# Second gate of the linear attention as a third seven-product block product, with adding DMAs for the weight sums

## The chip, the cores and the metric

The kernel runs on one NeuronCore of a Trainium2 chip. The metric is the device time of one execution in microseconds (us). TensorE (PE) multiplies matrices into PSUM; VectorE (DVE) and ScalarE (ACT) work elementwise on SBUF and PSUM; GpSimd (POOL) works on SBUF and issues DMAs; SyncE (SP) only issues DMAs. PEld is TensorE's loading of weights. All engines run their own instruction streams in order and wait for each other through semaphores.

## The reference, cut to what matters

One transformer block in float32 on 512 tokens of width 1024. One large projection gives all inputs; the change concerns the gate `z_ma`, which scales the output of the gated linear attention.

```python
n = rmsnorm(h, g_mix[l])
proj = n @ w_in[l]
(gq, gk, gv, gr, z_gf, z_gb, cq, ckv, kr, z_ma, z_mb) = jnp.split(proj, SPLIT_IDX, axis=-1)
y_gla = gla_branch(gq, gk, gv, gr, z_gf, z_gb, ...)     # ends with: rmsnorm(o, g_gla) * silu(gr)
y_mla = mla_branch(cq, ckv, kr, positions, ...)
merged = jax.nn.sigmoid(z_ma) * y_gla + jax.nn.sigmoid(z_mb) * y_mla
h = h + merged @ w_out[l]
m = rmsnorm(h, g_mlp[l])
h = h + jnp.square(jax.nn.relu(m @ w_ff1[l])) @ w_ff2[l]
```

`gr`, `gv` and `z_ma` are each 512 x 1024 (x 1024 inner). `gq` and `gk` are 512 wide (four heads of 128), `z_mb` is 1024 wide.

## The kernel before

**Precision.** Every float32 operand is split into a high part in the type fp32r (ACT, a copy) and a low part (DVE, source minus high part). A product of two operands is then three matmuls (`mm3`, line 430: high-high, high-low, low-high). `split` (435) is the pair of operations; `halves` (558) gives the two tiles for a weight block, of which there are four pairs (128 x 1024 each).

**Two ways to project.** A plain projection (`proj_begin`, `proj_run`) takes 128 columns of `w_in`: eight inner blocks of `mm3` over 512 tokens, 24 matmuls; its result stands with features on the partitions and tokens along the row. `gr` and `gv` instead go through `Seven` (1028): the 512 x 1024 times 1024 x 1024 product is cut in 2 x 2 blocks and computed with seven block products in place of eight (the Strassen-Winograd scheme). A block product is a 256 x 512 by 512 x 512 product, again 24 matmuls (four inner blocks, two token blocks, three terms), and its result has tokens on the partitions. The left sums (of the tokens' activations) are made once (`x_sums`, 998, on POOL; `split_sums`) and shared. The right sums (of weight blocks) are made by DVE in `less` (1043), subtracting one 128 x 1024 tile from another, two tiles per sum, four sums per block product. Before that, `load` (1033) brings all four weight blocks, two tiles of 512 KB each, over SP's queue. `right_split` splits a sum into halves. `multiply` (1076) runs the products and evacuates them: products 1, 5 and 6 are copied from PSUM by ACT into the rows c11, c22 and c12, products 2, 3 and 7 are added onto them by DVE. `sinks` (1102) hands finished rows on: `gr_rows` makes silu(gr) into `g1`, `gv_rows` makes the split values `v`.

**The gate before.** `z_ma` is computed by eight plain projections (`begin_za`, 1486). `za_gate` (1125) multiplies the result by the token rows' norm `R` (DVE), takes tanh (ACT) and scales and shifts by the gain `gla_gain` (ACT, bias and scale), since sigmoid(x) = (1 + tanh(x/2))/2. The linear attention's output of a head, gated by `g1` in `gla_gated`, is transposed in `gla_turn` (1151) and there multiplied by that gate (DVE).

**The order of the work.** From `nc.keep()` (1478) to `nc.flush` (2441) nothing is emitted at once: all operations are recorded, and `Due.order` (295) lays them out. It gives each operation a cost (`Work.cost`, 158) and a landing delay, works out a latest time for each from the order of the matmuls in the program, and then picks for each engine the ready operation that is due first. TensorE may take a matmul out of its order if that is due less than 6 us after the first one outstanding. Tiles of tags `u2` (24 buffers), `u4` (30), `wh`/`wl` (4) and the PSUM tags `mm` and `at` (4 banks each) put further limits on the order, since a new tile waits for the last use of an old one.

**Around the change.** The recorded part begins with the two sevens (gr, then gv). `prepare` for a product stands two steps ahead of it in the program. Filling projections (zb4, the gate and rotary-key projection zk, gq1, gk1, zb5) stand between products. Then come the heads h = 0, 1, 2 of the linear attention in a loop (1575): transposes of the keys (`turned`), `queries`, `scores`, one za projection, `values` (kv), `states` (a chain over four blocks of tokens, on ACT and DVE), another za projection, the output product `out`, squares and gating, the next head's q and k projections, and `gla_turn`. The gates' logarithms, scans and exponentials for the next head run meanwhile. The last head (1617) is mixed with the latent projections ckv and cq and the rotary parts, and with za6 and za7. Attention, the output product and the feed-forward part follow; these already form their weight sums with DMAs that add onto a tile (`nc.gpsimd.dma_start(..., accum_op=ALU.add)`), which POOL issues.

The steps of the sevens, before:

```python
SEVEN = (1, 2, 5, 6, 3, 7, 4)
steps = [(a, m) for a in range(2) for m in SEVEN]
```

Of the kernel before, what the change touches and what calls it, by code (L numbers as in the profile page):

```python
# [141 lines left out]
class Work:  # L142
    def __init__(self, engine, name, args, named):
# [8 lines left out]
        self.big = [n for x, n in zip(views, sizes) if not any(x is o for o in outs) and n > 4]  # L152
# [5 lines left out]
    def cost(self):  # L158
# [8 lines left out]
        if self.engine == "scalar":  # L167
            table = self.func not in (None, AF.Copy, AF.Identity, AF.Square)
            return 0.085 + 0.00086 * n + (0.02 if table else 0) + (0.11 if "accum_out" in self.named else 0)
        if self.engine == "vector":  # L170
            if self.name == "tensor_scan" or "scan" in self.name:
# [21 lines left out]
class Script:  # L193
# [4 lines left out]
    def __init__(self, nc, after):  # L198
        self.nc, self.after = nc, after
        self.kept, self.slots, self.last, self.used, self.count = None, {}, {}, {}, 0  # L200
        for e in self.ENGINES:
            setattr(self, e, Queue(self, e))
# [5 lines left out]
    def takes(self, held):  # L208
        held.real()
        if held.bufs is not None:  # L210
            here = self.slots.setdefault(held.kind, [])
            if len(here) == held.bufs:
                here.remove(min(here, key=lambda h: self.used.get(h, -1)))
            here.append(held)

    def told(self, work):
        self.count += 1
        for s in work.outs + work.ins:
            self.used[s[0]] = self.count
# [27 lines left out]
class Due:  # L247


    def __init__(self, todo, slots, head=0.0, tables=None):  # L250
# [4 lines left out]
        for i, w in enumerate(todo):  # L255
            for s in w.outs + w.ins:
                users.setdefault(s[0], []).append(i)
        wrote, read, seen, past = {}, {}, set(), {}
# [36 lines left out]
    def order(self):  # L295
# [4 lines left out]
            (9.4 if w.engine == "gpsimd" and w.bytes > 4e5 else 2.2) if w.is_dma else 0.13 for w in todo  # L300
# [30 lines left out]
        table = None  # L331
        self.idle = 0.0
        for _ in range(n):
            best = None
            for e in Script.ENGINES:
                among = open_[e]
                if e == "tensor" and among:
                    among = [i for i in among if late[i] < late[pe[-1]] + 6.0]
# [3 lines left out]
                i = min((i for i in among if ready[i] <= t + 0.1), key=lambda i: (late[i], i))  # L342
# [41 lines left out]
def tile_block(ctx: ExitStack, tc: tile.TileContext, t, out: bass.AP):  # L384
# [607 lines left out]
    SEVEN = (1, 2, 5, 6, 3, 7, 4)  # L992
# [5 lines left out]
    def x_sums():  # L998
        add = nc.gpsimd.tensor_tensor
        half = KD // 2  # L1000
        for p in range(half):
            a, b = xraw[p], xraw[p + half]
            y = u2(f"xy{p}")
            add(y[:, LO], a[:, HI], b[:, HI], op=ALU.add)
# [6 lines left out]
        for p in range(half):  # L1011
# [3 lines left out]
            add(z[:, HI], b[:, LO], x_y[p][:, HI], op=ALU.subtract)  # L1015
# [12 lines left out]
    class Seven:  # L1028
        def __init__(self, col, name, sink):
            self.col, self.name, self.sink = col, name, sink  # L1030
            self.blocks, self.right = [None] * 4, {}

        def load(self, x):

            self.blocks[x] = [u4(f"{self.name}w{x}{g}", F32, (P, 2, S)) for g in range(2)]
            for g in range(2):
                r = ((x // 2) * 4 + 2 * g) * P
                c = self.col + (x % 2) * S
                nc.sync.dma_start(
                    self.blocks[x][g], w_in[r : r + 2 * P, c : c + S].rearrange("(k p) w -> p k w", p=P)  # L1040
                )

        def less(self, dst, x, y):
            for g in range(2):
                nc.vector.tensor_tensor(
                    self.blocks[dst][g], self.blocks[x][g], self.blocks[y][g], op=ALU.subtract
                )
# [12 lines left out]
        def right_split(self, m, g):  # L1060
            x = {1: 0, 2: 2, 5: 0, 6: 0, 3: 3, 7: 1, 4: 2}[m]
# [14 lines left out]
        def multiply(self, m):  # L1076
# [5 lines left out]
            elif m == 5:  # L1082
                self.zs = [ps("at", f"{self.name}z{rb}") for rb in range(2)]
# [11 lines left out]
            if m in (1, 5, 6):  # L1095
                for acc, c in zip(accs, {1: self.c11, 5: self.c22, 6: self.c12}[m]):
                    nc.scalar.activation(c, acc, AF.Copy)
            elif m in (2, 3, 7):
                for acc, c in zip(accs, {2: self.c11, 3: self.c12, 7: self.c22}[m]):
                    nc.vector.tensor_tensor(c, acc, c, op=ALU.add)  # L1100

        def sinks(self, m):
# [3 lines left out]
            elif m in (2, 3, 7):  # L1106
                for rb, c in enumerate({2: self.c11, 3: self.c12, 7: self.c22}[m]):
# [15 lines left out]
    za_gates, held = {}, {}  # L1123
# [27 lines left out]
    def gla_turn(h):  # L1151

        half, at = h // 2, (h % 2) * GDV
        for dv in range(2):
# [6 lines left out]
            y = za_gates.pop(f)  # L1161
            nc.vector.tensor_tensor(y, tp, y, op=ALU.mult)
# [323 lines left out]
    def begin_za(f):  # L1486
        return begin(C_ZA + f * P, f"za{f}")
# [8 lines left out]
    def finish_zb(f, begun):  # L1496
        gated(proj_run(begun, xT), f"b{f}")


# [3 lines left out]
        (1, 2): (lambda: begin_qk(1, 0), lambda w: finish_qk(1, 0, w)),  # L1503
    }
    steps = [(a, m) for a in range(2) for m in SEVEN]
# [5 lines left out]
    for n, (a, m) in enumerate(steps[:-4]):  # L1511
        ahead = steps[n + 2]
        if a == 0:
# [956 lines left out]
```

## Time and profile before

| | us |
|---|---|
| median of 3 runs | 751.42 (750.8 to 752.75) |
| the profiled execution's own time | 752.12 |
| its span | 750.4 |
| TensorE's mean granted clock in it | 0.995 of full speed |

All instructions go through one helper line (L230), so groups are told apart by the names of the tiles. A group's row shows: engine, operation, out<-in, partitions x elements and type, count, busy time and mean duration in ns of one, then the engine's idle time just ahead and what ended it. Names: gr, gv, za, zb, gq, gk, ckv, cq with an h or l at the end are weight halves; grw, gvw the weight blocks; grx, grz, gvx, gvz accumulators of the sevens; kv the state products, st the states, glaNo the output product of head N, tr the tanh for silu. In the sections on the chain a piece is its start, its length and the engine.

### The profile page before, as it was taken

The numbers are of one execution on the slowest core, as the hardware profiler recorded it, in microseconds if no ns is written. First come the engines' busy times: TensorE is split into PE (matmuls) and PEld (weight loads), VectorE is DVE, ScalarE is ACT, GpSimd is POOL, SyncE is SP. The second block draws the span as 40 slices with busy tenths as digits, with TensorE's granted clock in tenths as the row PEclk, the third lists the DMA queues.
The fourth block names the chain that finished last, engine by engine and source line by source line (L and its number), as shares of the span: only waits on it lengthen the run. The fifth ranks groups of instructions, "written<-read, shape, count | busy, mean of one in ns | idle before, by whom it ended". The sixth has DMA issues, their size and how long they took to land.

```text
span 750.4 us, 11537 instructions
## 1 busy us (share of the span) xinstructions
PE 737.1 (98%) x4256; PEld 648.3 (86%) x4256; DVE 618.0 (82%) x920; ACT 503.7 (67%) x831; POOL 198.0 (26%) x243
## 2 busy tenths in 40 slices
PE   8999999999999999999999999999999999999996
PEld 6888788888888888899888899889988998889985
DVE  6699997887788486999997899857986798778885
ACT  7466649597776366988965768645873597458754
POOL 1540002113212104137743202322122211312433
PEclk9999999999999999999999999999999999999998
DMA  9931211413332316129975549998989897988992
GB/s 311 344 110 49 77 29 28 113 36 81 82 85 57 50 43 165 39 81 237 236 219 85 140 113 216 217 214 205 211 177 217 203 206 179 212 219 195 198 167 112
DMA packets 105176, 111.79 MB, mean 149 GB/s; under 512 B 15792, under 2 KB 75200, under 8 KB 105120
## 3 DMA queue, kind: packets, MB, share of 16 engines
q1 hardware_dynamic: 80976, 74.59, 32.9%
q0 software_dynamic: 23856, 35.94, 29.0%
q8 instruction: 33, 0.54, 0.3%
q10 hardware_dynamic: 288, 0.52, 0.2%
q14 instruction: 23, 0.19, 0.1%
HBM read 107.37 MB, written 2.10 MB: 146 GB/s over the span
## 4 chain that ended last, share of the span: by engine, by line
PE 85%; DVE 7%; ACT 3%; POOL 2%; issue 1%; DMA 1%; SPq 0%; POOLq 0%; DVEq 0%; ACTq 0%
PE mb L230 22%; PE ab L230 16%; PE za L230 6%; PE zb L230 4%; PE wox L230 3%; PE f L230 3%; PE gvx L230 3%; PE first L230 2%; PE grx L230 2%; PE cq L230 2%; PE gq L230 2%; PE gk L230 2%; PE ckv L230 1%; PE gvz L230 1%; PE woz L230 1%
## 5 line engine op out<-in xcount | busy, mean ns | idle before, releaser
L230 POOL DMA_DIRECT2D ms<-in_w_ff x37 | 47.3, 1372 | 115.5 <-DVE hl3l L230 37.5
L230 POOL DMA_DIRECT2D w1s<-in_w_ff x18 | 22.7, 1264 | 94.0 <-DVE hl0l L230 38.9
L230 DVE TENSOR_TENSOR h<-h,ab 128x512 f32<-128x512 f32 x48 | 31.7, 682 | 5.5 <-PE ab L230 5.5
L230 ACT ACTIVATE row<-row 128x512 f32<-128x512 f32 x49 | 30.7, 626 | 1.9 <-DVE row L230 1.0
L230 PE MATMUL av<-pT,v 128*128 128x256 f32 x192 | 28.2, 290 | 0.6 <-DVE pT L230 0.6
L230 PE MATMUL s<-kbuf,q 96*128 96x512 f32 x96 | 28.6, 409 | 0.0
L230 PEld LDWEIGHTS av<-pT,v 128*128 128x128 f32 x192 | 24.7, 191 | 1.2 <-DVE pT L230 0.8
L230 ACT ACTIVATE e<-s,top 128x512 f32<-128x512 f32 x32 | 21.9, 686 | 5.5 <-DVE top L230 5.2
L230 PE MATMUL mb<-four,hl0h 128*128 128x256 f32 x128 | 23.4, 284 | 0.1
L230 DVE TENSOR_REDUCE top<-s 128x1 f32<-128x512 f32 x32 | 21.5, 682 | 1.0 <-PE s L230 0.8
L230 DVE TENSOR_TENSOR pT<-tp,pT 128x512 fp32r<-128x512 f32 x32 | 21.5, 681 | 0.7 <-ACT pT L230 0.7
L230 DVE TENSOR_TENSOR hl3l<-ms,hl3h 128x1024 fp32r<-128x1024 f32 x13 | 15.9, 1224 | 7.0 <-ACT hl3h L230 6.8
L230 ACT ACTIVATE row<-mb 128x512 f32<-128x512 f32 x28 | 16.3, 582 | 7.3 <-PE mb L230 7.3
L230 PE MATMUL mb<-four,hl3h 128*128 128x256 f32 x112 | 20.5, 284 | 0.4 <-ACT row L230 0.4
L230 PEld LDWEIGHTS mb<-four,hl0h 128*128 128x128 f32 x128 | 20.1, 192 | 0.8 <-ACT hl2h L230 0.5
L230 PE MATMUL tp<-ident,e 128*128 128x128 f32 x128 | 19.5, 275 | 1.3 <-DVE pT L230 1.2
L230 ACT ACTIVATE hl3h<-ms 128x1024 fp32r<-128x1024 f32 x13 | 13.7, 1056 | 10.2 <-PE ab L230 4.6
L230 DVE TENSOR_TENSOR hl1l<-ms,hl1h 128x1024 fp32r<-128x1024 f32 x12 | 14.7, 1224 | 7.0 <-ACT hl1h L230 6.8
L230 PE MATMUL mb<-m,hl2h 128*128 128x256 f32 x112 | 20.4, 283 | 0.0
L230 PE MATMUL mb<-four,hl2h 128*128 128x256 f32 x112 | 20.4, 283 | 0.0
L230 PEld LDWEIGHTS tp<-ident,e 128*128 128x128 f32 x128 | 14.9, 140 | 5.5 <-PE s L230 1.5
L230 ACT ACTIVATE pT<-tp 128x512 fp32r<-128x512 f32 x32 | 19.0, 594 | 0.9 <-PE tp L230 0.8
(1097 smaller groups left out, 2815.4 us busy)
## 6 DMA issues: line engine op xcount, KB each, us to landing
ms<-in_w_ff POOLq DMA_DIRECT2D x37, 512.0 KB, 6.9
w1s<-in_w_ff POOLq DMA_DIRECT2D x18, 512.0 KB, 6.6
ms<-in_w_ff SPq DMA_DIRECT2D x16, 512.0 KB, 4.9
w1s<-in_w_ff SPq DMA_DIRECT2D x15, 512.0 KB, 4.7
w<-in_w_out POOLq DMA_DIRECT2D x10, 512.0 KB, 7.7
wf0f<-in_w_ff SPq DMA_DIRECT2D x10, 512.0 KB, 5.8
wf1f<-in_w_ff SPq DMA_DIRECT2D x10, 512.0 KB, 5.9
wf2f<-in_w_ff SPq DMA_DIRECT2D x10, 512.0 KB, 5.3
```

What stands on the lines that cost most here:

```text
L230: return call(*map(real, work.args), **{k: real(v) for k, v in work.named.items()})
```

## The change

- A third `Seven` for `z_ma` (named za) stands between gr and gv; its sink `za_rows` takes tanh by token rows, with the norm as ACT's scale, and multiplies 1 + tanh into `g1` (DVE). The eight plain za projections and `za_gate` go. `gla_turn` now only scales by the gain: ACT for one of a head's two parts, DVE for the other.
- The weight sums of all three sevens are formed by adding DMAs on POOL's queue (`by = "dma"`), onto B11 (three sums) and B22 (one). Block B12 has no tile of its own any more. The signs of the left sums and of the evacuations follow: product 3 is now copied into c12 and product 6 subtracted from it.
- The seven's inner order is now 1, 2, 5, 3, 6, 7, 4, and the list of steps interleaves the last products of a block with the first of the next. The accumulators of products 5 and 3 take banks of the tag `mm` instead of `at`.
- The fillers gq1 and gk1 stand in the last seven. zb5 moves into the first head; the second za projection's place in a head is taken by the next q projection; the first za place stays empty in heads 1 and 2. The first head's gate work stands in the last two steps of gv.
- The planner: new cost formulas, ACT's landing delay 0.145, TensorE may reach 20 us ahead instead of 6, ties within 0.05 us instead of 0.1, the activation table is known from the start, and tile slots are followed only for tiles with recorded uses.

```diff
 class Work:
+        sources = [*args[1:], *(x for k, x in named.items() if k != "accum_out")]
+        self.big = [x for x in sources if isinstance(x, View) and x.cells.size > 4]
+        self.from_psum = any(x.held.tag in ("mm", "at") for x in self.big)
...
         if self.engine == "scalar":
-            return 0.085 + 0.00086 * n + (0.02 if table else 0) + (0.11 if "accum_out" in self.named else 0)
+            more = (0.03 if table else 0) + (0.1 if "accum_out" in self.named and n > 256 else 0)
+            return more + (0.217 + 0.000543 * n if self.from_psum else 0.09 + 0.000857 * n)
...
-            extra = 0.055 if self.name == "scalar_tensor_tensor" and not self.psum else 0
-            return 0.07 + extra + (0.00105 if two or self.psum or self.name == "tensor_reduce" else 0.00066) * n
+            if self.name == "scalar_tensor_tensor":
+                return 0.125 + 0.00105 * n if not self.psum else 0.17 + 0.00085 * n
+            return 0.065 + (0.00105 if two or self.psum or self.name == "tensor_reduce" else 0.00066) * n
...
-                    among = [i for i in among if late[i] < late[pe[-1]] + 6.0]
+                    among = [i for i in among if late[i] < late[pe[-1]] + 20.0]
...
-                i = min((i for i in among if ready[i] <= t + 0.1), key=lambda i: (late[i], i))
+                i = min((i for i in among if ready[i] <= t + 0.05), key=lambda i: (late[i], i))
...
     class Seven:
-        def less(self, dst, x, y):
-            for g in range(2):
-                nc.vector.tensor_tensor(
-                    self.blocks[dst][g], self.blocks[x][g], self.blocks[y][g], op=ALU.subtract
-                )
+        def more(self, dst, x):
+            for g in range(2):
+                to = self.blocks[dst][g]
+                if self.by == "dma":
+                    nc.gpsimd.dma_start(to, self.rows(x, g), accum_op=ALU.add)
+                else:
+                    nc.vector.tensor_tensor(to, to, self.blocks[x][g], op=ALU.add)
 
         def right_sums(self, m):
             if m == 5:
-                self.less(0, 1, 0)
+                self.more(B11, B12)
             elif m == 6:
-                self.less(0, 3, 0)
-            elif m == 3:
-                self.less(2, 2, 0)
+                self.more(B11, B22)
             elif m == 7:
-                self.less(1, 3, 1)
+                if self.by == "dma":
+                    self.more(B22, B12)
+                else:
+                    self.more(B12, B22)
+            elif m == 4:
+                self.more(B11, B21)
...
             elif m == 5:
-                self.zs = [ps("at", f"{self.name}z{rb}") for rb in range(2)]
+                self.zs = [ps("mm", f"{self.name}z{rb}") for rb in range(2)]
...
-            if m in (1, 5, 6):
+            if m in (1, 5, 3):
...
-            elif m in (2, 3, 7):
+            elif m in (2, 6, 7):
...
-    def za_gate(f, acc):
-
-        z = u2(f"za{f}")
-        nc.vector.tensor_tensor(z, acc, R, op=ALU.mult)
-        nc.scalar.activation(z, z, AF.Tanh, scale=0.5)
-        gain = gla_gain[:, f : f + 1]
-        nc.scalar.activation(z, z, AF.Identity, bias=gain, scale=gain)
-        za_gates[f] = z
+    def za_rows(i, half, src, dst):
+        nc.scalar.activation(dst, src, AF.Tanh, scale=r_half[:, i : i + 1])
+        g = g1[i, half]
+        nc.vector.scalar_tensor_tensor(g, dst, 1.0, g, op0=ALU.add, op1=ALU.mult)
...
-            y = za_gates.pop(f)
-            nc.vector.tensor_tensor(y, tp, y, op=ALU.mult)
+            y = u2(f"y1{f}")
+            gain = gla_gain[:, f : f + 1]
+            if dv:
+                nc.vector.tensor_scalar(y, tp, gain, None, op0=ALU.mult)
+            else:
+                nc.scalar.activation(y, tp, AF.Copy, scale=gain)
...
-    sevens = [Seven(C_GR, "gr", gr_rows), Seven(C_GV, "gv", gv_rows)]
-    for x in (0, 2, 1, 3):
+    sevens = [Seven(C_GR, "gr", gr_rows, "dma"), Seven(C_ZA, "za", za_rows, "dma"), Seven(C_GV, "gv", gv_rows, "dma")]
+    for x in (B11, B21, B22):
         sevens[0].load(x)
...
-    steps = [(a, m) for a in range(2) for m in SEVEN]
+    steps = [(0, 1), (0, 2), (0, 5), (0, 3), (0, 6), (1, 1), (0, 7), (1, 2), (0, 4), (1, 5), (1, 3), (1, 6),
+             (2, 1), (1, 7), (2, 2), (1, 4), (2, 5), (2, 3), (2, 6), (2, 7), (2, 4)]
...
+        if a < 2:
+            for x in {2: (B11,), 5: (B21,), 6: (B22,)}.get(m, ()):
+                sevens[a + 1].load(x)
...
     for h in range(GH - 1):
         lin.turned()
         lin.queries()
         lin.scores()
-        if h:
-            w_b = begin_za(2 * h + 1)
-        acc = proj_run(w_a, xT)
+        if h == 0:
+            finish_zb(5, w_a)
...
         lin.states(coefs)
         gate.sums("f")
         if h < 2:
+            finish_qk(h + 2, 0, w_a)
             w_k, lows = begin_late(C_GK + (h + 2) * P, f"gk{h + 2}")
         else:
+            ckv_.run(0)
             ckv_.begun[1], lows = begin_late(C_CKV + P, "ckv1")
         gate.sums("b")
-        past, acc = acc, proj_run(w_b, xT)
         os = lin.out()
...
-    za_gate(6, proj_T(C_ZA + 6 * P, "za6"))
     lin.values()
     lin.states(coefs)
     cq = cq_.normed()
-    za_gate(7, proj_T(C_ZA + 7 * P, "za7"))
```

More of the change, by code (lines that the diff above doesn't have):

```diff
@@ L199, in __init__ @@
         self.nc, self.after = nc, after
-        self.kept, self.slots, self.last, self.used, self.count = None, {}, {}, {}, 0
+        self.kept, self.slots, self.last = None, {}, {}
         for e in self.ENGINES:
@@ L210, in takes @@
         if held.bufs is not None:
[L211 to L214, printed above, removed]
+            self.slots.setdefault(held.kind, []).append(held)
     def told(self, work):
-        self.count += 1
-        for s in work.outs + work.ins:
-            self.used[s[0]] = self.count
         if self.kept is not None:
@@ L330, in order @@
         shares = [w.shares() for w in todo]
-        table = None
+        table = 1
         self.idle = 0.0
@@ L1510, in tile_block, with prepare @@
     begun = {}
-    for n, (a, m) in enumerate(steps[:-4]):
-        ahead = steps[n + 2]
-        if a == 0:
-            for x in {3: (0,), 7: (2, 1), 4: (3,)}.get(m, ()):
-                sevens[1].load(x)
-        if steps[n + 1] in fillers:
+    for n, (a, m) in enumerate(steps):
+        ahead = steps[n + 2] if n + 2 < len(steps) else None
+        def prepare():
+            if ahead:
+                sevens[ahead[0]].prepare(ahead[1])
+        if a < 2:
+            for x in {2: (B11,), 5: (B21,), 6: (B22,)}.get(m, ()):
+                sevens[a + 1].load(x)
+        if n + 1 < len(steps) and steps[n + 1] in fillers:
             begun[steps[n + 1]] = fillers[steps[n + 1]][0]()
@@ L1525, in tile_block @@
             nc.gpsimd.dma_start(pos_i, t["positions"][0].partition_broadcast(P))
-        if (a, m) == (0, 4):
+        if (a, m) == (0, 7):
             z_chunk_finish(z_acc)
             split_gates()
+        if (a, m) == (2, 7):
+            gate = Gates(0)
+            gate.logs()
+        if (a, m) == (2, 4):
+            gate.sums("f")
+            gate.exps("f")
+            gate.sums("b")
+            gate.exps("b")
         if (a, m) in fillers:
             sevens[a].product(m)
-            sevens[ahead[0]].prepare(ahead[1])
+            prepare()
             rest = fillers[a, m][1](begun.pop((a, m)))
@@ L1600, in tile_block @@
         gate.exps("b")
-        za_gate(2 * h + 1, acc)
         gla_gated(h, os, rs)
```

83 lines of the change are left out of this document (27 added, 56 removed).

## The prediction

> **What bounds the kernel now.** I read the busy table first, then the chain of waits, then busy time by stage, then the groups and pieces that the change touches.
>
> ```profile
> span 750.4 us, 11537 instructions
> PE 737.1 (98%) x4256; PEld 648.3 (86%) x4256; DVE 618.0 (82%) x920; ACT 503.7 (67%) x831; POOL 198.0 (26%) x243
> PE 85%; DVE 7%; ACT 3%; POOL 2%; issue 1%; DMA 1%; SPq 0%; POOLq 0%; DVEq 0%; ACTq 0%
> ```
>
> TensorE is busy for 737.1 of 750.4 us and holds 85% of the chain. So only two things can move the time: the number of matrix products, and what opens or closes a gap between them. The stages say where gaps could open (columns: stretch, its length, then busy time and count of PE, weight loads, DVE, ACT, POOL, then clock, DMA share, GB/s).
>
> ```profile
> 43.40:146.00 102.60, 102.39 (x451) 84.29 (x450) 94.40 (x111) 65.33 (x86) 11.16 (x20) 1.00 0.22 59
> 146.00:297.20 151.20, 151.20 (x824) 131.11 (x823) 114.87 (x220) 106.21 (x200) 32.79 (x62) 1.00 0.29 73
> 297.20:381.00 83.80, 81.86 (x554) 73.07 (x553) 77.56 (x134) 72.48 (x160) 43.12 (x50) 1.00 0.65 164
> 360.00:381.00 21.00, 19.67 (x140) 17.25 (x140) 20.13 (x37) 18.97 (x43) 16.97 (x19) 1.00 0.98 255
> 480.00:730.00 250.00, 250.00 (x1576) 227.03 (x1575) 200.41 (x264) 155.78 (x208) 60.54 (x51) 1.00 0.94 201
> 730.00:750.40 20.40, 13.65 (x72) 11.62 (x70) 11.49 (x19) 8.99 (x20) 8.09 (x12) 0.89 0.28 103
> 297.20:750.40 453.20, 443.50 (x2818) 400.15 (x2816) 378.35 (x545) 304.63 (x501) 135.25 (x134) 0.99 0.79 180
> ```
>
> From 43.4 to 146 run the two seven-product blocks (gr and gv); from 146 to 297.2 the four heads of the linear attention with the eight za projections as filling; then attention. In the linear stage TensorE has no gap at all, with DVE at 114.87/151.20 = 76% and ACT at 70%. Attention, with DVE at 92.5% and ACT at 86.5%, leaves TensorE idle for 1.94 us of 83.8 (2.3%); its last quarter, DVE at 95.9%, for 1.33 of 21 (6.3%). The granted clock is 1.00 in all stages that the change touches, so no term below is a clock.
>
> **The change, part by part.**
>
> *Matrix products.* The chain shows one projection or one of the seven products as 24 matmuls:
>
> ```profile
> 43.75 5.44 PE grx L230 x24
> ...
> 149.43 5.47 PE za L230 x24
> 154.90 2.15 PE kv L230 x18
> 157.05 5.47 PE za L230 x24
> 162.52 3.59 PE gla0o L230 x30
> 166.11 5.47 PE gq L230 x24
> ```
>
> Eight za projections of 24 matmuls go, seven products of 24 come. One unit is 5.44 us, so TensorE loses 8 - 7 = 1 unit: **-5.44 us**. This is on the path, since TensorE is. No other matmul or transpose is added.
>
> *Work of DVE and ACT.* Rows (out<-in, shapes, count, busy us, mean ns, idle before):
>
> ```profile
> L230 DVE TENSOR_TENSOR gvw<-gvw,gvw 128x1024 f32<-128x1024 f32 x8 | 9.8, 1220 | 0.1
> L230 DVE TENSOR_TENSOR grw<-grw,grw 128x1024 f32<-128x1024 f32 x8 | 9.4, 1219 | 0.0
> L230 DVE TENSOR_TENSOR za<-za,R 128x512 f32<-128x512 f32 x8 | 5.5, 686 | 1.0 <-PE za L230 1.0
> L230 DVE TENSOR_TENSOR za<-y,za 128x512 f32<-128x512 f32 x8 | 5.3, 685 | 0.2
> L230 DVE TENSOR_TENSOR gv20l<-gvw,gv20h 128x1024 fp32r<-128x1024 f32 x1 | 1.2, 1218 | 0.0
> L230 DVE SCALAR_TENSOR_TENSOR grb<-tr,grb 128x512 f32<-128x512 f32 x2 | 1.3, 689 | 0.0
> L230 DVE TENSOR_SCALAR mf<-gatef,gvec 128x512 f32<-128x512 f32 x4 | 3.0, 748 | 0.6 <-PE gatef L230 0.6
> L230 ACT ACTIVATE za<-za,gla_gain 128x512 f32<-128x512 f32 x8 | 6.5, 813 | 0.2
> L230 ACT ACTIVATE za<-za 128x512 f32<-128x512 f32 x8 | 5.0, 626 | 0.6 <-DVE za L230 0.5
> L230 ACT ACTIVATE tr<-grb,r_half 128x512 f32<-128x512 f32 x2 | 1.3, 708 | 0.0
> L230 ACT ACTIVATE za2h<-za2f 128x1024 fp32r<-128x1024 f32 x1 | 1.1, 1062 | 0.1
> ```
>
> In the seven-product stage DVE loses the 16 differences of weights (9.8 + 9.4 = 19.2 us), the lows of za0, za1 (they lie before 146, about 2 x 1.2) and of zb5 (1.2), and gains 14 lows of the za block at 1.22 (17.1), 6 additions and 8 gate products at 0.69 (9.6): 94.4 - 22.8 + 26.7 = 98 us. TensorE there has 102.4 + 7 x 5.44 - 5.44 (zb5 moves on to the first head) = 135 us. DVE falls from 92% to 73%. ACT gains 14 highs at 1.06, 6 copies of accumulators (bounded by 0.6 to 0.8, the two rows za<-za and za<-za,gla_gain) and 8 tanh at 0.71 and loses 3 highs: 65 + 15 + 4 + 6 - 3 = 87 of 135 us. Neither bounds; all of it lies beside the products.
>
> In the linear stage the filling goes: TensorE 151.2 - 8 x 5.46 + 5.44 = 113 us. DVE loses six lows (7.3), eight scalings (5.5), six turned products (4.1; the last head's two lie in attention), and gains zb5's low (1.2) and three scalings out of PSUM at 0.75 (2.2; the other half goes to ACT): 114.9 - 16.9 + 3.4 = 101.4 us, **90% of TensorE's time instead of 76%**. ACT: 106.2 - 6.5 - 5.0 - 6.3 + 1.1 + 2 = 91.5, 81%. This is where a gap must be expected. Between the two rows for density (76%: no gap; attention's 92.5%: 2.3% of gap) 89.8% reads as 1.9% of 113 us: **+2.2 us**. Bounds: 0 (the row of before; no gain is possible in a stage without a gap) and 6.3%, the densest quarter of attention, 7.1 us. I take 2.2 because attention, with its chains of transpose, split and evacuation, is the row most like it.
>
> *The adding DMAs.* 24 transfers of 512 KB through POOL (four sums of two halves, three blocks) come; of the plain loads 18 stay for the blocks against 16 and eight for za.
>
> ```profile
> ms<-in_w_ff POOLq DMA_DIRECT2D x37, 512.0 KB, 6.9
> w1s<-in_w_ff POOLq DMA_DIRECT2D x18, 512.0 KB, 6.6
> gvw<-in_w_in SPq DMA_DIRECT2D x8, 512.0 KB, 6.1
> L230 POOL DMA_DIRECT2D ms<-in_w_ff x37 | 47.3, 1372 | 115.5 <-DVE hl3l L230 37.5 <-DVE hl0l L230 34.2 <-DVE hl1l L230 17.0
> DMA to landing us min/median/max: 3.7/6.6/15.4
> ```
>
> An issue costs POOL 1.37 us, 33 us in all, beside only 11 us of other POOL work in that stage. A sum then takes 1.4 + 6.9 us where DVE took 1.22, and it has to wait until the split before it has read the block. Is it in time? There are four pairs of halves and a product uses two, so the split for a product starts when the product two places ahead frees its half. For the tightest pair, product 5 and then 6 with one between: if 5 starts at t, its second half is split by t - 5.4 + 1.06 + 1.22 = t - 3.2, the first by t - 5.9. Product 6 starts at t + 10.9 and needs its first half split (2.3 us) by then, so the sum may take until t + 8.6: 14.5 us from the issue, against 6.9. **Cost 0.** The cover is the two products between; if it were gone, each microsecond beyond 14.5 would cost one, three times. The feed-forward stage supports the value: 250 us at 201 GB/s and 60 us of POOL, most of it such transfers, without a gap on TensorE, while the new stage would move some 41 x 0.52 MB in 135 us, 160 GB/s. Behind a waiting add on POOL stand the next add, the clearing of the scan rows and the small gate copies; the next add is the only urgent one, and one product of delay (5.4) still leaves 12.3 under 14.5. On SP's queue the loads of the next block wait for free tiles ahead of zb and gq weights; there were 16 + 8 such loads before and 18 now, so I cost it at 0 too.
>
> *The order elsewhere.* The new cost formulas, the window of 20 us for TensorE and the new tie limit lay every stage after the marker anew. From 297.2 to 730 TensorE idles 9.7 - 6.75 = 2.95 us; a new order could win or lose about half of it: -1.5 to +1.5, taken as 0. Swapping products 6 and 3, the changed signs and the bank for product 5 change no count.
>
> **Sum.** The profiled execution took 752.12 us, 0.70 above the median of the runs shown (751.42). 752.12 - 5.44 + 2.2 = 748.9; less 0.70: **748.2 us**. Its own range, with the order elsewhere, is 746.5 to 750.
>
> **The rivals.**
>
> *Everything stays covered.* No gap opens in the linear stage: 752.12 - 5.44 - 0.70 = 746.0. For it: the planner may now reach 20 us ahead for a ready matmul, and the next stage (zb6, cq) has DVE to spare. Against: 90% is close to attention's density. Chance 0.22.
>
> *The linear stage gets as tight as the end of attention.* Gap 7.1 us, 746.0 + 7.1 = 753.1. For it: per head the products shrink by about 10.9 us but the chain of scans, exponentials and states doesn't. Against: DVE has slack before (73%) and after. Chance 0.18. The Trainium skill (Perfetto Trace Analysis, Optimization Strategy) advises interleaving regimes whose most-contended engines differ; this change takes products without DVE work out of the DVE-heavy stage, so by that rule this rival is the likely one. The trace agrees as far as it goes: no gap at 76%, 2.3% at 92.5%.
>
> *The states lie bare (slower).* In one head the state products end at 157.05 and the last state is split at 161.54 + 0.54:
>
> ```profile
> 161.54 0.54 DVE L230 SCALAR_TENSOR_TENSOR st<-wf,e3f,st 128x256 fp32r<-128x256 f32 x1 [0.35 <-ACT st L230]
> ```
>
> These 5.0 us were covered by a za projection; now a q projection must do it, whose weight halves come from the same busy DVE. If they come late in three heads, 15.0 us lie open: 746.0 + 15.0 = 761.0. It decides from 7.7 us on (half of it), where 751.42 + 0.3% is reached. Against: the rest of zb5, gk and the following projections are ready candidates too. Chance 0.12.
>
> *The adds come late.* At the longest landing seen, 15.4, each block loses 15.4 - 14.5 = 0.9, three times 2.7: 750.9. Against: the median is less than half. Chance 0.06. The Trainium skill (SBUF — State Buffer, A bandwidth-pool intuition that's wrong) gives about 0.62 us alone and 3.1 us beside a VectorE copy for a DMA issued from GpSimd; 2.5 us more would make 9.4 of the 6.9, by which this rival still doesn't come.
>
> **How the numbers follow.** Forecast 0.42, rivals 0.22, 0.18, 0.12 and 0.06. A measurement of this kernel tells 0.3%, 2.25 us, from no change, so faster means below 749.2 and slower above 753.7. Faster: all of 0.22, 0.34 of the forecast's 0.42, 0.01 of the late adds, 0.57. Slower: the bare states' 0.12 and 0.07 of the tight stage, 0.19. Within: 0.24. The range runs from 745.2 (all covered, and half of what the order elsewhere could give) to 754.0 (the tight stage and a little); it leaves out the bare states and small tails of the others.
>
> **What would show it.** In the changed profile: 24 fewer matmuls on TensorE and about 5.4 us less between 43 and 300, whatever the time does. Seven-product stage: no TensorE gap, DVE near 73%, POOL near 33% with waits for DVE lows, adds landing in about 7 us; waits of splits for a DMA would prove the late adds. Linear stage: a length near 113 + 2 us, with gaps at the first scores or the output product of a head; gaps of about 5 us after the state products, ended by a split of st, would prove the bare states. Attention and feed-forward: idle as before within 1.5 us. The prediction is wrong if the stage from 146 on shows DVE near 99%, if attention's gap changes by more than 2 us, or if TensorE waits for weights in the sevens.

## The result, and the profile after

| | before | after |
|---|---|---|
| median, us | 751.68 (14 runs) | 750.13 (14 runs, 749.19 to 750.75) |
| ratio with its 95% interval | | 0.9979 (0.9971 to 0.9987) |
| the profiled execution's own time, us | 752.12 | 749.19 |

The change gains 1.55 us (1.0 to 2.2 by the interval), about half of the 3.2 that the prediction gave (748.2 against 751.42). The two profiled executions differ by 2.93 us, nearly twice as much: that of before was 0.44 above the median of its kernel, that of after is the fastest of its 14 runs, and 0.79 us lie ahead of the first gr product (it starts at 43.59 before and at 42.80 after). So I compare the traces from that product on: to the last product of the kernel they take 699.8 us before and 697.8 after, 2.0 us less.

The busy table and the shares of the chain of waits, kernel after:

```profile
span 747.4 us, 11565 instructions
PE 732.9 (98%) x4232; PEld 643.2 (86%) x4232; DVE 607.8 (81%) x912; ACT 507.7 (68%) x839; POOL 228.9 (31%) x267
PE 75%; ACT 11%; DVE 8%; POOL 3%; issue 2%; DMA 1%; POOLq 0%; SPq 0%; ACTq 0%; DVEq 0%
```

TensorE has 4232 products instead of 4256: the 24 that were to go are gone. But its share of the chain fell from 85% to 75% and ScalarE's rose from 3% to 11%. A chain that runs through ScalarE is one in which TensorE waits, or is only just served.

Busy time by stage, kernel after (columns as in the prediction; the first row is the three blocks, the second the four heads, then attention, then the feed-forward part):

```profile
42.80:178.70 135.90, 135.82 (x597) 111.39 (x596) 97.28 (x116) 83.92 (x108) 44.74 (x42) 1.00 0.72 148
178.70:297.20 118.50, 116.13 (x670) 101.08 (x669) 105.02 (x207) 92.04 (x189) 37.34 (x71) 1.00 0.26 57
297.20:381.00 83.80, 81.79 (x541) 71.86 (x541) 77.22 (x135) 72.37 (x160) 43.62 (x52) 1.00 0.71 184
480.00:727.00 247.00, 247.00 (x1564) 224.78 (x1563) 198.63 (x262) 154.85 (x207) 60.40 (x50) 1.00 0.93 203
```

The stage of the blocks is full: 0.08 us idle in 135.90. The heads are not: 2.37 us idle where before had none. Busy time of pipelined products covers small stalls, so I also took the start-to-start times of TensorE's products out of both traces. Each product has a steady distance to the next (0.227 us for 512 columns, 0.120 for 256, 0.109 for a 128x128 transpose or score; 0.231 for attention's scores), and what a stage takes beyond the sum of these is lost time. This is a calculation of mine from the starts, and no view shows it:

| from, to | steady before | lost before | steady after | lost after |
|---|---|---|---|---|
| first gr product, first turn of head 0 | 102.5 | 0.77 | 135.1 | 0.84 |
| first turn, first score of attention | 152.5 | 0.62 | 114.4 | 4.86 |
| attention | 84.2 | 3.80 | 84.2 | 4.36 |
| output projection and first part of feed-forward | 73.5 | 1.53 | 73.5 | 0.83 |
| rest of feed-forward | 278.7 | 1.77 | 278.7 | 1.02 |

Steady work falls by 5.4 us. Lost time rises by 4.2 in the heads and 0.6 in attention, and falls by 1.45 in the feed-forward stages: -5.4 + 0.1 + 4.2 + 0.6 - 1.45 = -2.0, the whole difference of the traces.

**The largest gap.** TensorE's waits between 43 and 297 us, kernel after (who waits, for whom, us in total, times, the longest); before had none there:

```profile
PE scb L228 <- DVE gv L228: 1.8, 1, 1.8
PE kv L228 <- ACT bds L228: 0.5, 1, 0.5
```

The first is the gap ahead of the first scores of head 0. TensorE there, kernel after (start, duration, instruction, idle time before it and who ended it):

```profile
178.07 0.39 PE L228 MATMUL gvx<-gv41h,xT 128*128 128x512 f32 x1
...
179.33 0.71 PE L228 MATMUL zb<-xT,zb5h 128*128 128x512 f32 x2
181.79 1.16 PE L228 MATMUL scb<-qkb 128*128 128x128 f32 x8 [1.75 <-DVE gv L228]
```

The score banks are those that gv's last product filled; they come free when gv is read out. VectorE makes gv's low part out of these banks, from the high part that ScalarE reads out of them first, and it waited for ScalarE, kernel after:

```profile
180.99 1.41 DVE L228 SCALAR_TENSOR_TENSOR gv<-gvx,r_x,gv 128x512 fp32r<-128x512 f32 x2 [1.94 <-ACT gv L228]
```

This is what ScalarE did, kernel after:

```profile
175.38 1.05 ACT L228 ACTIVATE gq2h<-gq2f 128x1024 fp32r<-128x1024 f32 x1
178.81 0.21 ACT L228 ACTIVATE e3b<-v3b 128x12 f32<-128x12 f32 x1 [2.38 <-POOL v3b L228]
178.93 1.04 ACT L228 ACTIVATE gk2h<-gk2f 128x1024 fp32r<-128x1024 f32 x1
179.88 0.50 ACT L228 ACTIVATE qsb<-qkb 128x384 fp32r<-128x384 f32 x1
180.29 1.25 ACT L228 ACTIVATE gv<-gvx,r_x 128x512 fp32r<-128x512 f32 x2
```

ScalarE stood for 2.38 us at a 0.21 us exponential of twelve columns, in order, with gk2h, qsb and the two read-outs of gv behind it. It waited for GpSimd, kernel after:

```profile
171.38 0.23 POOL L228 COPY v3f<-rrf 128x4 f32<-128x4 f32 x1 [20.34 <-DVE rrf L228]
...
172.64 5.85 POOL L228 COPY v3b<-rrb 128x4 f32<-128x4 f32 x1 [0.39 <-DVE rrb L228]
178.45 0.20 POOL L228 TENSOR_TENSOR v3b<-rrb 128x4 f32<-128x4 f32 x1
178.59 0.18 POOL L228 COPY v3b<-rrb 128x4 f32<-128x4 f32 x1
```

A copy of four columns took 5.85 us; its like for the other direction took 0.23 just before. What VectorE did meanwhile, kernel after:

```profile
173.08 0.68 DVE L228 TENSOR_TENSOR difb<-rrb 128x512 f32<-128x512 f32 x1
173.68 1.22 DVE L228 TENSOR_TENSOR zb5l<-zb5f,zb5h 128x1024 fp32r<-128x1024 f32 x1
...
177.22 1.22 DVE L228 TENSOR_TENSOR gq2l<-gq2f,gq2h 128x1024 fp32r<-128x1024 f32 x1
178.36 0.69 DVE L228 TENSOR_TENSOR gkn<-gk,R 128x512 f32<-128x512 f32 x1
```

Operations whose operands both lie in SBUF, end to end, until gkn, which reads gk out of PSUM. The copy ends at 178.49, within 0.05 us of the end of gq2l.

In the kernel before the same spot was covered. TensorE of the kernel before, from gv's last product to the first scores:

```profile
140.70 0.39 PE L230 MATMUL gvx<-gv41h,xT 128*128 128x512 f32 x1
140.93 0.62 PE L230 MATMUL zb<-xT,zb5h 128*128 128x512 f32 x2
...
147.48 1.06 PE L230 MATMUL scb<-qkb 128*128 128x128 f32 x8
```

There 6.8 us of work (the zb5 projection, gates and turns) lay between the two. The change lets zb5 run among head 0's products, nearly all of it behind the scores. From gv's last product at 178.07 to where the scores could have started, behind the two products of zb, only 1.8 us are left to read the banks out; they started 3.7 us behind it.

### The profile page after: what moved, and what is told of

Its sections match the earlier page's. It is cut to its first block, busy times and chain, and to the rows that moved or that the text cites. A ratio compares the mean times of both kernels' runs of the same rounds, so it can differ in the third digit from the quotient of the medians.

```text
span 747.4 us, 11565 instructions
## 1 busy us (share of the span) xinstructions
PE 732.9 (98%) x4232; PEld 643.2 (86%) x4232; DVE 607.8 (81%) x912; ACT 507.7 (68%) x839; POOL 228.9 (31%) x267
## 4 chain that ended last, share of the span: by engine, by line
PE 75%; ACT 11%; DVE 8%; POOL 3%; issue 2%; DMA 1%; POOLq 0%; SPq 0%; ACTq 0%; DVEq 0%
PE mb L228 23%; PE ab L228 16%; PE zb L228 3%; PE zax L228 3%; PE grx L228 3%; PE f L228 3%; PE wox L228 3%; PE first L228 2%; PE cq L228 2%; PE gvx L228 2%; ACT e L228 2%; PE grz L228 1%; PE gvz L228 1%; PE woz L228 1%; PE zaz L228 1%
## 5 line engine op out<-in xcount | busy, mean ns | idle before, releaser
L228 ACT ACTIVATE hl1h<-ms 128x1024 fp32r<-128x1024 f32 x12 | 12.7, 1059 | 10.9 <-PE ab L228 4.8
```

The lines of the kernel that those rows point to most:

```text
L228: return call(*map(real, work.args), **{k: real(v) for k, v in work.named.items()})
```

## The experiments

All ratios are to the kernel before, run on the same chip as the experiment. "Lost" is the calculation of the table above.

**e1: the new planner alone.** The kernel before, with nothing changed but the planner: its costs, ACT's landing delay, the reach, the tie limit, the activation table and the tile slots. Two of the changes:

```diff
-                    among = [i for i in among if late[i] < late[pe[-1]] + 6.0]
+                    among = [i for i in among if late[i] < late[pe[-1]] + 20.0]
...
-                i = min((i for i in among if ready[i] <= t + 0.1), key=lambda i: (late[i], i))
+                i = min((i for i in among if ready[i] <= t + 0.05), key=lambda i: (late[i], i))
```

> The kernel of before with the changed cost formulas, TensorE's reach of 20 us and the tie limit of 0.05 us, and nothing else of the change. Theory (the block product's gain is lost in the linear stage, and the stages from attention on give about 1 us through the new order): 0.5 to 1.5 us under the kernel before, with no TensorE gap between 43 and 297 us and less idle between 422 and 460. Rival (the order elsewhere is worth nothing and the differences between the two profiles there are chance): within 0.4 us of the kernel before.

Measured: 751.38 against 751.61, ratio 0.9996 (0.9987 to 1.0005). The feed-forward stages lose 1.5 us less, attention 1.7 more. Most of the latter is one wait in attention, TensorE of e1:

```profile
365.22 0.81 PE L228 MATMUL tp<-ident,e 128*128 128x128 f32 x4 [1.79 <-DVE tot L228]
```

What follows: the new planner gains and loses alike on the old work. The total is that of the rival, but not for its reason: the 1.5 us in feed-forward is there, and attention takes it back. The 1.45 us that after saves in feed-forward is theirs.

**e2: the change with the old planner.** The kernel after, with the planner's lines of before put back (e1's diff the other way round).

> The changed kernel laid out with the formulas, the reach of 6 us and the ties of the kernel before. Theory: the gain of 5.4 us is lost in the same place, and the 1 us from the order elsewhere goes as well, so 0.5 to 2 us over the changed kernel. Rival (the reach of 20 us is what keeps the linear stage from losing more): 3 us or more over the changed kernel, with the added gaps in the heads.

Measured: 754.98, ratio 1.0046 (1.0033 to 1.0059), about 5 us above after. Lost time rises over that of after by 1.3 us in the blocks, 1.3 in the heads, 1.5 in attention and 1.5 in feed-forward. TensorE's waits in e2 between 43 and 297 us:

```profile
PE scb L230 <- DVE gv L230: 1.3, 1, 1.3
PE grw L230 <- DVE gr20l L230: 0.9, 1, 0.9
...
```

What follows: the loss is the rival's 3 us or more, but only 1.3 of it lies in the heads where the rival put it. With the old planner the change costs time; it needs the new one, which alone is worth nothing. The wait at the first scores is there under both, so it isn't an accident of the new order.

**e3: the small columns on VectorE.** The kernel after, with the three operations for v3 taken from GpSimd:

```diff
-            nc.gpsimd.tensor_copy(v3[:, 0, :], rr[:, :, 64])
-            nc.gpsimd.tensor_tensor(v3[:, 1, :], rr[:, :, P], rr[:, :, 64], op=ALU.subtract)
-            nc.gpsimd.tensor_copy(v3[:, 2, :], rr[:, :, P])
+            nc.vector.tensor_copy(v3[:, 0, :], rr[:, :, 64])
+            nc.vector.tensor_tensor(v3[:, 1, :], rr[:, :, P], rr[:, :, 64], op=ALU.subtract)
+            nc.vector.tensor_copy(v3[:, 2, :], rr[:, :, P])
```

> In the changed kernel the three small operations per direction and head that fill v3 from the scans' rows run on VectorE instead of GpSimd. Theory (in the changed kernel GpSimd's copy of v3b took 5.85 us while VectorE worked through a row of operations with two SBUF operands; ScalarE stood behind it, and gv's last accumulators left their banks late, so the first scores waited 1.8 us): each small operation takes under 0.2 us, ScalarE's wait for v3b and the gap before the first scores go, 1.5 to 2.5 us under the changed kernel. Rival (the stage is too dense, the gap only moves on): within 0.5 us of the changed kernel. Second rival (the wait is for zb5's place, not for GpSimd): the gap at the first scores stays.

Measured: 748.56, ratio 0.9962 (0.9949 to 0.9974). From the first gr product to the end the trace takes 696.9 us, 0.8 less than after. ScalarE at the same place in e3:

```profile
177.59 1.24 ACT L228 ACTIVATE gv<-gvx,r_x 128x512 fp32r<-128x512 f32 x2
...
181.29 0.21 ACT L228 ACTIVATE e3b<-v3b 128x12 f32<-128x12 f32 x1 [0.23 <-DVE v3b L228]
```

The two read-outs of gv no longer stand behind e3b and run 2.0 us earlier (counted from the first gr product), and the first scores start with no wait. But a wait appears where head 0's gated output is transposed (`gla_turn`), TensorE of e3:

```profile
204.45 0.72 PE L228 MATMUL y<-ident,gra 128*128 128x128 f32 x2 [1.16 <-DVE gra L228]
```

What follows: the chain is shown: the read-outs were late because they stood behind e3b, which waited for GpSimd's copy. It is ScalarE's order that helped and not an earlier v3b: VectorE began v3b only at 180.55, 2.5 us later than GpSimd had finished it in after (178.77), counted from the first gr product, but the planner now laid e3b behind the read-outs. Lost time in the heads falls only from 4.86 to 3.84, and the gain over after stays under the expected 1.5 to 2.5 us; 1.2 us turn up as the wait at that turn of head 0. Whether that is the rest of the same cost isn't shown.

**e4: zb5 back in its old place.** The kernel after, with zb5 between gv's last product and head 0; the copies stay on GpSimd:

```diff
+        (2, 4): (lambda: begin(C_ZB + 5 * P, "zb5"), lambda w: finish_zb(5, w)),
...
-    w_a = begin(C_ZB + 5 * P, "zb5")
...
-        if h == 0:
-            finish_zb(5, w_a)
```

> In the changed kernel the projection zb5 stands again between gv's last product and the first head, as before the change, instead of after the first scores. Theory (ScalarE's place behind GpSimd's copy is the cause, and 5.4 us of projection cover any such wait): the gap before the first scores goes, but the first head then has no projection between scores and state products and loses part of it there: 0 to 1.5 us under the changed kernel. Rival (density decides, so one place of filling is as good as another): within 0.4 us of it.

Measured: 748.56, ratio 0.9965 (0.9952 to 0.9977); the trace from the first gr product on takes 696.5 us, 1.3 less than after. TensorE of e4:

```profile
178.39 0.39 PE L228 MATMUL gvx<-gv41h,xT 128*128 128x512 f32 x1
178.61 0.61 PE L228 MATMUL zb<-xT,zb5h 128*128 128x512 f32 x2
...
185.16 1.06 PE L228 MATMUL scb<-qkb 128*128 128x128 f32 x8
```

The wait at the scores is gone here too. But ScalarE no longer stood at e3b either: the copy took 2.31 us in place of 5.85 (rows in the last section), and the read-outs of gv start 0.39 us behind gv's last product in place of 2.22. ScalarE of e4:

```profile
177.72 0.20 ACT L228 ACTIVATE e3b<-v3b 128x12 f32<-128x12 f32 x1
```

What follows: putting zb5 back takes the wait away, but the run doesn't separate its cover from the shorter copy that came with it. That the cover alone would do is an estimate from the rows: even in after the scores started 3.7 us behind gv's last product, and in e4 6.8 us of work lie there. Lost time in the heads is 3.5 us. The intervals of e3 and e4 reach up to 0.9974 and 0.9977 and that of after begins at 0.9971, so the gain of either over after, 1.0 to 1.3 us by the ratios, is not sharp in size.

**e5: both.** The kernel after with the edits of e3 and e4.

> The changed kernel with the small v3 operations on VectorE and zb5 back between gv's last product and the first head. Theory (both remove the same gap of 1.9 us, and after that about 3 us of thinly spread gaps stay in the heads): 1.5 to 2.5 us under the changed kernel, 3 to 4 us under the kernel before, hardly better than either alone. Rival (two separate gaps): the sum of both, 3 us or more under the changed kernel.

Measured: 748.17 against 751.30, ratio 0.9960 (0.9947 to 0.9973); 697.0 us from the first gr product on, 3.5 lost in the heads. By the trace no better than either alone, as it must be if both remove one and the same gap. It has the lowest ratio of all versions run, though its interval overlaps those of e3 and e4, and by a hair that of after.

**e6: the weight sums by VectorE.** The kernel after, with the 24 sums as additions of loaded blocks:

```diff
-    sevens = [Seven(C_GR, "gr", gr_rows, "dma"), Seven(C_ZA, "za", za_rows, "dma"), Seven(C_GV, "gv", gv_rows, "dma")]
+    sevens = [Seven(C_GR, "gr", gr_rows, "dve"), Seven(C_ZA, "za", za_rows, "dve"), Seven(C_GV, "gv", gv_rows, "dve")]
```

> The changed kernel with the weight sums of all three block products as VectorE additions of loaded blocks in place of adding DMAs: 24 additions of 1.22 us, 29 us more for VectorE, which then has 126 of some 136 us in the block products. Theory (the adding DMAs are hidden and only relieve VectorE): the block products are still bound by TensorE up to small gaps, 0 to 3 us over the changed kernel. Rival (VectorE was the bound to be of the third block product): 5 us or more over it.

Measured: 749.27, ratio 0.9978 (0.9968 to 0.9988), the same as after. The stage of the blocks in e6:

```profile
42.80:178.70 135.90, 135.90 (x600) 111.73 (x599) 123.69 (x142) 84.97 (x108) 9.07 (x11) 1.00 0.25 71
```

What follows: the adding DMAs take 26.4 us off VectorE (123.69 to 97.28) and put 35.7 on GpSimd, and neither shows in the time, where the intervals of e6 and after, 0.6 to 0.8 us to either side, lie on each other: at 91% VectorE still lies wholly beside TensorE. GpSimd's copy of v3b took 5.85 us in e6 as well, and the first scores waited 2.1.

**e7: two blocks only.** The kernel after with the eight za projections back in the heads and two blocks instead of three; adding DMAs, interleaved products and the planner stay.

> The changed kernel without the third block product: gr and gv by adding DMAs and in the interleaved order, za again by eight plain projections in the heads, za_gate and zb5 as before. Theory (only the product count and the gaps in the heads count): no gap between 43 and 297, so within 1 us of the kernel before, and the linear stage as long as before (151 us). Rival (adding DMAs and interleaving are worth something by themselves): 2 us or more under the kernel before.

Measured: 751.68, ratio 1.0000 (0.9989 to 1.0010); lost in the heads 0.62, as before. What follows: adding DMAs, interleaved products and the planner together are worth nothing within 0.8 us. The whole gain comes with the third block, which does seven products for eight, and so does the opening of the heads.

**e8: GpSimd copies beside VectorE operations.** The kernel after, with three rows of eight VectorE operations behind its end, each with three small GpSimd copies beside it (two SBUF operands; one operand in PSUM; one in SBUF with a scalar).

> The changed kernel with a probe behind its end: GpSimd makes three small copies of 4 columns while VectorE runs eight operations, first with two SBUF operands (128x512), then with one operand in PSUM and one in SBUF (128x128), then with one SBUF operand and a scalar (128x512). Theory (GpSimd gets no turn while VectorE goes from one operation with two SBUF operands to the next): in the first round one copy takes most of the 4.8 us of the eight operations, in the second all take under 0.3 us each. Rival (the 5.85 us copy waited for something else): all copies under 0.5 us in each round. The probe adds some 12 us to the time, which says nothing.

GpSimd and VectorE in e8 (the first two forms, and the last copy of the third):

```profile
744.85 4.90 DVE L228 TENSOR_TENSOR ptwo<-pb,pc 128x512 f32<-128x512 f32 x8
745.00 1.18 POOL L228 COPY probetwo<-pa 128x4 f32<-128x4 f32 x2 [2.25 <-DVE pa L228]
746.12 0.66 POOL L228 COPY pa<-probetwo 128x4 f32<-128x4 f32 x1
750.41 0.31 POOL L228 COPY probebank<-pa 128x4 f32<-128x4 f32 x2 [3.63 <-DVE pa L228]
750.65 0.19 POOL L228 COPY pa<-probebank 128x4 f32<-128x4 f32 x1
753.31 0.46 POOL L228 COPY pa<-probeone 128x4 f32<-128x4 f32 x1
```

What follows: beside two SBUF operands a copy takes 0.66 us, about one VectorE operation (0.68), and beside one SBUF operand and a scalar 0.46 (operations of 0.48); only beside an operand in PSUM does it take 0.19. So it isn't the second SBUF operand alone that slows a copy. Neither expectation came: none was held over a row, and not all stayed under 0.5.

**e9: the real stretch rebuilt.** As e8, with scans, difference and lows in the kernel's sizes and the copies out of strided columns.

> After the kernel's last operation the stretch from the scans to the lows is rebuilt on VectorE: four scans, one difference, then six operations of 1024, 512, 512, 512, 512 and 1024 columns. Beside the six GpSimd copies three columns of four numbers out of the scans' rows, as the kernel before head 0's scores does. Four forms: two operands in SBUF and strided columns; the same with four neighbouring numbers; one operand in SBUF and strided columns; two operands in pieces of 128 columns. Theory one, the copy is held back until the row of two-operand operations ends: the first copy of the first form takes 3 us or more, ends when the row ends, and is below 1 us in the third form. Theory two, a copy is slowed but never held over a row: 0.2 to 1.2 us in the first form too, and the 5.85 us stays unexplained. If the stride matters, form two stays below 1 us where form one is long. If what counts is that VectorE's operations are long, form four is shorter than form one. The time is that of the changed kernel and some 20 to 40 us for the added work.

GpSimd in e9 (first, third and fourth form), with VectorE's row of the first:

```profile
747.56 1.91 POOL L228 COPY v3twocol<-rrtwocol 128x4 f32<-128x4 f32 x3 [4.76 <-DVE rrtwocol L228]
761.07 1.44 POOL L228 COPY v3onecol<-rronecol 128x4 f32<-128x4 f32 x3 [6.56 <-DVE rronecol L228]
766.05 0.98 POOL L228 COPY v3narrow<-rrnarrow 128x4 f32<-128x4 f32 x3 [3.11 <-DVE rrnarrow L228]
```

```profile
748.22 4.75 DVE L228 TENSOR_TENSOR po<-pb,pb 128x1024 fp32r<-128x1024 f32 x6
```

What follows: theory two. One by one in the trace, the three copies of the first form took 0.19, 0.64 and 1.20 us; the last two end within 0.05 us of the end of the VectorE operation beside them, the difference and the first of 1024 columns. The third form has the same with one operand in SBUF (0.72 beside an operation of 0.74), and beside operations of 128 columns a copy took 0.26. That a copy stays behind for eight operations wasn't reproduced. Whether the stride matters this run doesn't tell: the copies of neighbouring numbers ran ahead of the row, beside the scans. What made the one copy last 5.85 us stays open.

## Why the prediction was right in its mechanism and off in its size

*Matrix products, -5.44 us.* Right: 24 products fewer, and steady work lower by 5.4.

*The stage of the blocks.* Right: 135.90 us long (135), VectorE at 97.28/135.90 = 72% (73%), ScalarE at 83.92 us (87), GpSimd at 33% (33%), no gap.

*The adding DMAs, 0.* Right. In the list of DMA issues of the kernel after (count, KB each, median us to landing) they land inside the 14.5 us that two products between leave them, the longest of these tiles' transfers in 10.9 us:

```profile
grw<-in_w_in POOLq DMA_DIRECT2D x8, 512.0 KB, 8.1
zaw<-in_w_in POOLq DMA_DIRECT2D x8, 512.0 KB, 8.2
gvw<-in_w_in POOLq DMA_DIRECT2D x8, 512.0 KB, 6.5
```

No product waited for a DMA in this stage. An issue took 1.2 us of GpSimd, by the groups of the kernel after (busy us, mean ns, then idle time and what ended it):

```profile
L228 POOL DMA_DIRECT2D grw<-in_w_in x8 | 9.6, 1217 | 14.8 <-DVE gr60l L228 4.9 <-DVE gr10l L228 4.8 <-DVE gr31l L228 2.0
```

The Trainium skill (SBUF — State Buffer, A bandwidth-pool intuition that's wrong) has a GpSimd-issued DMA held up beside a VectorE copy. Beside a VectorE busy for 72% of this stage, the mean issue took less here than the 1.37 us of before, and the median landings lie at most 1.3 us above the 6.9 costed; no run here tells how much of a landing, if any, is such a hold.

*The gap in the heads, +2.2 us.* **This is the term that was mis-sized: 4.2 us were lost.** The density that I worked from came out nearly as forecast (VectorE 105.02/118.50 = 89%, against 90%; ScalarE 78%, against 81%), and the largest gap lies where the last part of the prediction looked for it, at the first scores. Two steps failed.

The first is the yardstick. The term took idle time of the busy table for time lost. In idle time it came out right: 2.37 us of 118.5, 2.0% against 1.9%. But the table misses what is lost inside the pipelined products: 4.86 us were lost in these heads, and 3.80 in the attention of before, whose 1.94 us of idle time the term was read from. Read between the same two rows in lost time (0.62 us in the heads of before, 3.80 in attention), the gap would have come out at about 3.5 us more than before; this is an estimate from my table of lost time. It lies between the 2.9 that stay without the wait told next and the 4.2 measured.

The second is a wait that no density knows, some 1.9 us: the change took a 5.44 us projection away between a product and the next use of its banks, and left a GpSimd copy, ScalarE's order and the read-out in a row. I had moved zb5's 5.44 us and its low in the sum, and never asked what zb5 had covered. e3 takes e3b out of the way of the read-outs and its trace gains 0.8; e4 puts zb5 back and gains 1.3. The 3.5 us that stay in the heads of e4 and e5 are several gaps under 0.9 us each; that is 2.9 more than before. So of the 2.0 us by which the term was short, about 1.3 go with the wait in e4 and e5 (1.0 in e3) and 0.7 stay.

*The order elsewhere, 0, within 1.5 us.* Right in size, not in balance: feed-forward -1.45, attention +0.6. e1 and e2 show that the planner is no bystander: without it the change loses 3.5 us, ratio 1.0046.

*The rivals.* The states didn't lie bare: no wait for st between 43 and 297 us. The adds weren't late. The heads came out between the forecast and the stage as tight as the end of attention (4.2 between 2.2 and 7.1). The Trainium skill (Perfetto Trace Analysis, Optimization Strategy) spoke for the latter; the trace agrees in the direction, for it is the heads that opened when their products without VectorE work went. Full cover fell.

Without the one wait the kernel reaches the forecast: 748.2 to 748.6 in e3, e4 and e5, against 748.2. Part of that is luck: in e4 the heads still lose 2.9 us more than before, not 2.2, and feed-forward's 1.45, which the sum had at 0, makes up for that and for attention's 0.6.

## What to carry to other kernels

When a change moves a piece of filling, list what finishes under it, not only what it costs where it lands: here the read-out of the banks that the very next product needs. A density tells whether small gaps will open, if the gaps of the rows it is read from are taken from start to start and not as idle time in a busy table; single waits are found by following, for each first use of a buffer, the engines in order in front of its release. And a small operation that needs a side engine's result should not stand ahead of a read-out of PSUM in the order of the engine that does both: here one of 0.21 us held the read-outs back.

## What the runs showed of the hardware that was not expected

A GpSimd copy of 128x4 numbers took 0.18 to 0.19 us when VectorE had an operand in PSUM and 0.23 to 0.37 beside scans. Beside operations that read only SBUF it lasted in e8 and e9 to the end of the operation running (0.26 to 1.20 us), with one SBUF operand and a scalar as with two. In five versions the copy of v3b ahead of head 0 took longer: 5.85 in after and e6, 4.72 in e2, 2.31 in e4 and e7. These copies too end where a VectorE operation ends. In e4, GpSimd and VectorE:

```profile
174.10 2.31 POOL L228 COPY v3b<-rrb 128x4 f32<-128x4 f32 x1 [0.39 <-DVE rrb L228]
176.36 0.68 POOL L228 TENSOR_TENSOR v3b<-rrb 128x4 f32<-128x4 f32 x1
176.98 0.65 POOL L228 COPY v3b<-rrb 128x4 f32<-128x4 f32 x1
```

```profile
175.14 1.22 DVE L228 TENSOR_TENSOR gq2l<-gq2f,gq2h 128x1024 fp32r<-128x1024 f32 x1
176.28 0.69 DVE L228 TENSOR_TENSOR qkf<-gkn,eef 128x512 f32<-128x512 f32 x1
176.90 0.69 DVE L228 TENSOR_TENSOR qkb<-gkn,eeb 128x512 f32<-128x512 f32 x1
```

The first copy ends at 176.41 with gq2l (176.36), having let two earlier ends pass; the next two end at 177.04 and 177.63, with one operation each (176.97, 177.59). The Trainium skill (SBUF — State Buffer, Who interferes with whom) says that a VectorE operation with two SBUF inputs and a GpSimd operation that reads SBUF exclude each other, and whichever issues second waits for the first. The ends agree with that. The order doesn't: in after the copy started at 172.64, ahead of difb at 173.08, and difb and six more operations went through before it. The same copy got in at the first end in e9, the third in e4, the seventh in e2 and the eighth in after. In e2 and after VectorE's next operation was one that reads PSUM (gv, gkn); in e4 it wasn't. No run here shows what decides.

The time to the first gr product varied from 41.4 to 43.6 us among the profiled executions of before, after, e3, e4 and e5, which compute the same up to there; that is more than the whole gain: single profiles are compared from a common point, and medians decide.
